# A two-layer hybrid decoder trunk under an offline planner: port lock for more VectorE operations, the silu product on VectorE, every sum of squares as a split pair

## The chip, the core and the metric

The kernel runs on one core of a Trainium2 chip, as one launch. The metric is the device time of that launch in microseconds (us), the median of several runs. The engines are named as the profile names them: PE is TensorE (PEld its weight loads), DVE is VectorE, ACT is ScalarE, POOL is GpSimd and SP is SyncE, which issues all DMAs here.

## What is computed

The trunk has two layers over 1024 positions and a width of 1024, all in float32. A layer normalises, projects into four token mixers (latent attention, gated convolution, causal pooling, sliding-window attention with sinks), normalises each group, projects out, adds, and then runs a SwiGLU feed-forward part. Cut to what the change touches:

```python
def rmsnorm(x, g):
    xf = x.astype(jnp.float32)
    y = xf * lax.rsqrt(jnp.mean(xf * xf, axis=-1, keepdims=True) + RMS_EPS)
    return (y * g.astype(jnp.float32)).astype(x.dtype)
...
for l in range(DEPTH):
    h = rmsnorm(x, attn_norm[l])
    proj = h @ w_in[l]
    ...            # y_a latent attention, y_b conv, y_c pooling, y_d sliding window
    groups = jnp.stack([y_a, y_b, y_c, y_d], axis=2)
    gf = groups * lax.rsqrt(jnp.mean(groups * groups, axis=-1, keepdims=True) + RMS_EPS)
    x = x + (gf.reshape(b, s, D_MIX) * mix_norm[l]) @ w_o[l]
    h2 = rmsnorm(x, ffn_norm[l])
    gate, up = jnp.split(h2 @ w_gate_up[l], 2, axis=-1)
    x = x + (jax.nn.silu(gate) * up) @ w_down[l]
return rmsnorm(x, final_norm)
```

## The kernel before

Activations lie transposed: channels on the 128 partitions, positions along the free axis in two halves of 512 (t = 0 and 1). All SBUF working tiles are halves or pairs of halves out of 47 slots; they are all called `u` in the profile. PSUM tiles (`ps_...`) are 512 float32 wide.

**Products.** Nearly every matmul is done on operands split into two fp32r parts. `split` writes the high part with a cast on ACT (L301) and the low part with a subtraction on DVE (L304); `mm3` (L281) then issues three matmuls for each product: high by high, high by low, low by high. A sum of squares over the channels needs no such product: class `SumSq` squares on ACT (L336, L345), adds on DVE (L353, L347), and `rnorm` multiplies the accumulator by a matrix of ones on PE. That last step is in one of two forms. With `pair=False` the ones and the accumulator are float32 and there is one matmul (L364). With `pair=True` the accumulator is split by L301 and L304, and there are two fp32r matmuls with `ones_r` (L361). What follows is the same: ACT takes logarithm, exponential and square (L370 to L372), DVE one Newton step (L373, L376).

**Stages of a layer.** The input projection feeds the sliding-window units, the convolution and the pooling; then the latent attention with the output projection between its heads; then `combine`, which makes the seven operands of a Strassen-like product for the feed-forward part (Winograd's form: seven half-size products in place of eight). Per block of 128 hidden channels the gate-up part makes sums of weight quarters on POOL (`sums`, L1234 to L1236, `sum4`, L1264), products on PE, and `silu(g, r)`: the sigmoid-weighted gate on ACT (L1477), and its product with the row scale r on POOL (L1479). Results go through DRAM (`ad`, `qd`), and the down part runs the seven products again, with weight sums by `dn_sum` (L1557) on POOL. `premake` (L770 to L773) makes the weight sums of two gate-up blocks early: eight POOL additions in each layer, while the sliding-window units run.

**A sliding-window unit** (`swa_unit`) is a chain through the engines: scores on PE (L594), bias and row minimum on DVE (L604), exponential on ACT (L617), three short DVE operations on the row sums (L627, L629, L630), the scaling of the probabilities on DVE (L632), transposes on PE (L643), and the product with the values (L655).

**What sets the order.** `scheduled_kernel` records the program, gives each instruction a modelled duration (`Order.costs`), and lists it on five queues, one for each engine and one for the DMAs. `_forward` plays the queues against each other; `find` makes a first order, `_search` tries random changes of rank and keeps one when the mean over four draws of DMA delays falls (1500 tries). The order found is imposed on each engine's queue; between engines only the true dependences hold. Buffers and PSUM banks are given out by the planned times, in five rounds. One rule in `_forward` is for the port that DVE and POOL share: an operation of kind `TWO` (DVE) or `POOL` starts once the lock is free, and holds it until about its end. Which DVE operations are of kind `TWO` is said in `Order.kinds`; before the change these are additions and products of two wide SBUF operands:

```python
two = op == "TensorTensor" or op == "TensorScalarPtr" and i.is_scalar_tensor_tensor
if e == "DVE" and two and len(aps) == 2:
    return 0 if any(a.memref.startswith("ps_") for a in aps) else TWO
```

Of the kernel before, what the change touches and what calls it, by code (L numbers as in the profile page):

```python
# [23 lines left out]
P = 128  # L24
D = 1024
# [105 lines left out]
def trunk_kernel(ctx: ExitStack, tc: tile.TileContext, ins, out, given=None, spans=None, made=None):  # L131
# [256 lines left out]
    x_in = ins["xT"]  # L388
    ss = SumSq(D)
    hh = [[None, None] for _ in range(NK)]  # L390
# [48 lines left out]
    for l in range(L):  # L439
# [254 lines left out]
        def group_scale(g):  # L694

            sg = SumSq(2 * P, g in "b")
            for t in range(2):
                for c in range(2):
                    sg.add(t, F.ap(y[g][c][t]))
                r = sg.rnorm(t)  # L700
                for c in range(2):
                    a = F.ap(y[g][c][t])
                    mul_to(a, a, F.ap(r))
                F.free(r)
# [137 lines left out]
        cq = [[None, None], [None, None]]  # L842
        sq_q = SumSq(2 * P)
        for m in range(2):
# [630 lines left out]
        def silu(g, r):  # L1475
            nonlocal last_silu
            last_silu = act.activation(g, g, AF.Silu)  # L1477
            behind(last_silu, ss2.last)
            pool.tensor_tensor(out=g, in0=g, in1=r, op=ALU.mult)  # L1479

# [397 lines left out]
def _forward(eng, kind, seen, taken, kb, want, late, hop, start, to, sync, count, rank, fixed, order):  # L1878
# [21 lines left out]
    for _ in range(n):  # L1900
# [45 lines left out]
        if kind[k] >= TWO:  # L1946
            get = max(t + 0.08, lock)
            more = get - t - 0.08
            lock = get + seen[k] - (0.16 if kind[k] == TWO else 0.19)
        elif e == ACT and want[k] >= 0:  # L1950
            if want[k] != table:
                more = 0.0 if kind[k] == TABLE else 1.29
                table = want[k]
# [68 lines left out]
@compiled  # L2022
def _trials(arrays, graph, lates, order):

    eng, kind, seen, taken, kb, want, hop = arrays
    start, to, sync, count = graph[:4]
    none = np.zeros(0)
    total = 0.0
    for s in range(lates.shape[0]):
        end, _, ok = _forward(  # L2030
            eng, kind, seen, taken, kb, want, lates[s], hop, start, to, sync, count, none, True, order
        )
        if not ok:
            return 1e18
        total += end.max()
    return total / lates.shape[0]


@compiled
def _search(arrays, graph, lates, margin, rank, trials, seed):  # L2040
# [11 lines left out]
    )  # L2052
    best = _trials(arrays, graph, lates, order)
    first = best
# [4 lines left out]
    for it in range(trials):  # L2059
# [57 lines left out]
        if e1.max() > end.max() + 1.5:  # L2117
            continue
        got = _trials(arrays, graph, lates, trial)
        if got < best:  # L2120
# [7 lines left out]
class Order:  # L2128
# [75 lines left out]
    def wide(cls, i):  # L2204
        return [a for a in i.ins if hasattr(a, "memref") and cls.size(a) > 2]

    @classmethod
    def table(cls, i):
# [7 lines left out]
    def kinds(cls, i):  # L2216
# [6 lines left out]
        if op == "TensorTensor" and e == "Pool":  # L2223
            return POOL
        two = op == "TensorTensor" or op == "TensorScalarPtr" and i.is_scalar_tensor_tensor
        if e == "DVE" and two and len(aps) == 2:
            return 0 if any(a.memref.startswith("ps_") for a in aps) else TWO
        return 0

    @classmethod  # L2230
    def costs(cls, i):
# [8 lines left out]
        if e == "PE":  # L2240
            if i.is_transpose:
                return 0.28, 0.109
            if i.ins[0].dtype == F32:
                return n * 0.002, n * 0.0017
            return 0.178 + n * 0.000417, 0.0133 + n * 0.000417
# [44 lines left out]

    def search(self, trials, seed=1):
        rank = self.find()[1]
        best, first, wins, rank, order, begin, end = _search(
# [44 lines left out]
def scheduled_kernel(fresh, ins_of, rounds=5, trials=TRIALS):  # L2338
# [20 lines left out]
    best = None  # L2359
    for _ in range(rounds):  # L2360
        _, _, begin, end = plan.find()
        given = plan.banks(begin, end), plan.spans(made, begin, end)
        nc, traced, made = trace(*given)
        plan = Order(traced, nc.dependency_edges)
        found = plan.find()[0]
        if best is None or found < best[0]:
            best = found, given, plan
    order = best[2].search(trials)[1]
    return trace(*best[1], order)[0]

# [132 lines left out]
```

## Time and profile before

| | before |
|---|---|
| median of 3 runs (lowest, highest) | 2063.58 us (2062.7, 2064.33) |
| the profiled execution, its own time | 2065.29 us |
| span of its instructions | 2063.5 us, 26530 instructions |
| PE busy | 2036.2 us, 9422 matmul records |
| DVE busy | 1564.7 us, 2443 instructions |
| ACT busy | 992.0 us, 1737 instructions |
| POOL busy | 568.5 us, 420 instructions |
| mean granted clock of PE | 0.995 |

The profiled execution is 1.7 us over the median of the runs. A float32 matmul of 512 columns stands in the trace as two records, a fp32r one as one. Matmuls overlap: a record lasts about 0.39 us, while a new one begins every 0.23 us, so the rate is read from the starts or from a count in a window. In the list of waits a row reads: who waited, on which line, for whom; total us, times, longest us. In a timeline a row reads: start, duration, engine, line, operation, tiles, shapes, count, and in brackets the idle time before it and who ended it.

### The profile page before, as it was taken

What the parts mean: (1) busy time and instruction counts of PE and PEld (TensorE: products, weight loads), DVE (VectorE), ACT (ScalarE), POOL (GpSimd) and SP (SyncE); (2) the same over time, 40 slices, a digit from 0 to 9 for tenths busy, and PEclk for the clock granted to TensorE, in tenths of its full rate; (3) what the DMA queues carried; (4) which work ended last, traced back from release to release, by engine and by line L of the source; (5) the groups of instructions that cost most, each with busy time, mean ns of one, the idle gap of its engine ahead of it and who ended that gap; (6) DMA issues with size and microseconds to landing.
All of it is one profiled execution on the core that took longest, in us unless ns stands there. A gap on an engine that the chain in (4) does not pass through costs nothing.

```text
span 2063.5 us, 26530 instructions
## 1 busy us (share of the span) xinstructions
PE 2036.2 (99%) x9422; PEld 1679.0 (81%) x9422; DVE 1564.7 (76%) x2443; ACT 992.0 (48%) x1737; POOL 568.5 (28%) x420
## 2 busy tenths in 40 slices
PE   9999999999999999999999999999999999999998
PEld 7787888778888888888887878888788888888887
DVE  8879978998777678655657899789876767785546
ACT  7447647753333334444434476577433333354332
POOL 0100000037687683000001000000578768710000
PEclk9999999999999999999999999999999999999999
DMA  5301222434555556766403002243355555486542
GB/s 207 128 21 36 76 81 83 160 105 169 183 181 172 182 184 240 260 218 222 160 31 125 31 25 89 67 128 118 109 191 175 184 182 178 165 310 239 186 161 100
DMA packets 142117, 302.36 MB, mean 147 GB/s; under 512 B 13856, under 2 KB 60960, under 8 KB 141984
## 3 DMA queue, kind: packets, MB, share of 16 engines
q1 hardware_dynamic: 141984, 300.66, 43.1%
q8 instruction: 74, 1.21, 0.2%
q14 instruction: 59, 0.48, 0.1%
HBM read 212.00 MB, written 87.56 MB: 145 GB/s over the span
## 4 chain that ended last, share of the span: by engine, by line
PE 87%; DVE 6%; ACT 3%; issue 2%; DMA 1%; POOL 0%; SPq 0%; DVEq 0%; ACTq 0%; POOLq 0%
PE ps_mm L281 34%; PE ps_s L281 26%; PE ps_t L281 10%; PE ps_pv L281 8%; PE ps_pv L1065 2%; PE ps_t L1053 1%; DVE u L304 1%; PE ps_s L999 1%; DVE u L307 1%; PE ps_s L1001 1%; PE ps_s L1000 1%; DMA u<-in_w_gu 1%; PE ps_s L871 1%; PE ps_pv L655 1%; ACT u L306 1%
## 5 line engine op out<-in xcount | busy, mean ns | idle before, releaser
L281 PE MATMUL ps_mm<-u,u 128*128 128x512 f32 (+1 forms) x3378 | 839.3, 391 | 4.2 <-DVE u L304 1.7
L281 PEld LDWEIGHTS ps_mm<-u,u 128*128 128x128 f32 x3378 | 618.5, 189 | 130.9 <-issue 5.4
L281 PE MATMUL ps_s<-u,u 128*128 128x512 f32 x2670 | 639.7, 390 | 3.1 <-ACT u L301 1.0
L304 DVE TENSOR_TENSOR u<-u,u 128x1024 fp32r<-128x1024 f32 (+2 forms) x400 | 477.3, 1210 | 167.7 <-ACT u L301 101.8
L281 PEld LDWEIGHTS ps_s<-u,u 128*128 128x128 f32 x2670 | 500.4, 188 | 112.1 <-ACT u L301 2.6
L301 ACT CAST u<-u 128x1024 fp32r<-128x1024 f32 (+2 forms) x400 | 346.8, 882 | 479.0 <-PE ps_s L281 121.5
L281 PE MATMUL ps_t<-u,u 128*128 128x512 f32 (+1 forms) x1124 | 255.8, 377 | 0.5 <-ACT u L306 0.5
L281 PEld LDWEIGHTS ps_t<-u,u 128*128 128x128 f32 x1124 | 202.7, 188 | 40.3 <-ACT u L306 1.3
L1479 POOL TENSOR_TENSOR tp<-tp,u 128x512 f32<-128x512 f32 x80 | 132.3, 1654 | 338.5 <-ACT tp L1477 338.5
L281 PE MATMUL ps_pv<-u,u 128*128 128x512 f32 x744 | 179.2, 389 | 0.1
L281 PEld LDWEIGHTS ps_pv<-u,u 128*128 128x128 f32 x744 | 139.5, 188 | 29.8 <-ACT tn L1342 0.6
L1062 POOL MEMSET u<- 128x128 f32 x32 | 5.7, 206 | 497.9 <-PE ps_mm L281 324.9
L770 POOL TENSOR_TENSOR u<-u,u 128x512 f32<-128x512 f32 x4 | 5.3, 1316 | 373.1 <-PE ps_s L594 288.1
L1477 ACT ACTIVATE tp<-tp 128x512 f32<-128x512 f32 x80 | 50.5, 632 | 109.1 <-DVE tp L380 108.9
L301 ACT CAST u<-ps_t 128x512 fp32r<-128x512 f32 (+3 forms) x132 | 64.4, 502 | 64.3 <-PE ps_t L643 30.1
L304 DVE TENSOR_TENSOR u<-ps_t,u 128x512 fp32r<-128x512 f32 (+3 forms) x132 | 74.5, 580 | 13.6 <-ACT u L301 12.7
L1264 POOL TENSOR_TENSOR u<-u 128x512 f32<-128x512 f32 x38 | 77.8, 2048 | 20.8 <-DVE u L304 20.8
L306 ACT ACTIVATE u<-u,par 128x512 fp32r<-128x512 f32 x100 | 69.8, 715 | 25.5 <-DVE u L380 11.8
L1557 POOL TENSOR_TENSOR u<-u 128x352 f32<-128x352 f32 x64 | 80.6, 1260 | 2.4 <-DMA u<-in_w_dn 1.3
L307 DVE SCALAR_TENSOR_TENSOR u<-u,par,u 128x512 fp32r<-128x512 f32 x100 | 72.9, 746 | 5.0 <-ACT u L306 4.8
L1557 POOL TENSOR_TENSOR u<-u,u 128x352 f32<-128x352 f32 x64 | 74.6, 1165 | 3.6
L345 ACT ACTIVATE tn<-u 128x512 f32<-128x512 f32 (+1 forms) x91 | 52.3, 595 | 43.3 <-DVE u L1750 41.0
(206 smaller groups left out, 2377.2 us busy)
## 6 DMA issues: line engine op xcount, KB each, us to landing
u<-in_w_gu SPq DMA_DIRECT2D x92, 512.0 KB, 3.6
ad<-u SPq DMA_DIRECT2D x154, 256.0 KB, 2.1
u<-ad SPq DMA_DIRECT2D x70, 512.0 KB, 5.8
u<-in_w_dn SPq DMA_DIRECT2D x64, 352.0 KB, 3.2
qd<-u SPq DMA_DIRECT2D x64, 352.0 KB, 3.0
u<-qd SPq DMA_DIRECT2D x32, 512.0 KB, 5.2
u<-in_w_in SPq DMA_DIRECT2D x28, 512.0 KB, 3.8
u<-in_w_dn SPq DMA_DIRECT2D x24, 512.0 KB, 6.5
```

Source lines behind the costliest of these rows:

```text
L281: pe.matmul(o, w, r, start=start and k == 0 and i == 0, stop=stop and k == n - 1 and i == 2, skip_group_check=again,)
L301: a = act.copy(hi, f)
L304: dve.tensor_tensor(out=lo, in0=f, in1=rd(hi), op=ALU.subtract)
L306: a = act.activation(hi, f, AF.Copy, scale=gain)
L307: dve.scalar_tensor_tensor(out=lo, in0=f, scalar=gain, in1=rd(hi), op0=ALU.mult, op1=ALU.subtract)
L345: act.activation(q, f, AF.Square)
L655: pe.matmul(py[:, (i % 2) * 256 : (i % 2 + 1) * 256], v, R.ap(tt)[:, kb * 256 : (kb + 1) * 256], start=n == 0, stop=n == 2 * nkb - 1,)
L1065: pe.matmul(py[:, c0:], v_of(j, h), R.ap(s)[:, c0:], start=j == 0 and n == 0, stop=j == nj - 1 and n == 1,)
L1264: pool.tensor_tensor(out=q4, in0=q4, in1=F.ap(self.raw[1] + 1), op=ALU.add)
L1477: last_silu = act.activation(g, g, AF.Silu)
L1479: pool.tensor_tensor(out=g, in0=g, in1=r, op=ALU.mult)
L1557: pool.tensor_tensor(out=o, in0=a, in1=b, op=ALU.add)
```

## The change

Three things are changed in what the kernel executes, and the planner around it:

- `SumSq` is built with `pair=True` everywhere: also for the first normalisation, for the groups c and d, and for the latent queries. The one remaining float32 form is the second half of the final normalisation, which `rnorm` takes in two column ranges of 256.
- The product in `silu` is a DVE instruction.
- The planner takes every DVE addition, product, scaling or copy whose tensor operands all lie in SBUF as kind `TWO`, whatever their width; a PE transpose is planned at 0.1135 us where it was 0.109; each of the five rounds is judged by a search of its own, and the last search starts from the best round's ranks. A trial that can no longer win is cut short.

```diff
-    ss = SumSq(D)
+    ss = SumSq(D, True)
...
-            sg = SumSq(2 * P, g in "b")
+            sg = SumSq(2 * P, True)
...
-        sq_q = SumSq(2 * P)
+        sq_q = SumSq(2 * P, True)
...
             behind(last_silu, ss2.last)
-            pool.tensor_tensor(out=g, in0=g, in1=r, op=ALU.mult)
+            dve.tensor_tensor(out=g, in0=g, in1=r, op=ALU.mult)
...
             more = get - t - 0.08
-            lock = get + seen[k] - (0.16 if kind[k] == TWO else 0.19)
+            lock = get + max(0.05, seen[k] - (0.16 if kind[k] == TWO else 0.19))
...
+    @staticmethod
+    def tensors(i):
+        return [a for a in i.ins if hasattr(a, "memref")]
...
-        two = op == "TensorTensor" or op == "TensorScalarPtr" and i.is_scalar_tensor_tensor
-        if e == "DVE" and two and len(aps) == 2:
-            return 0 if any(a.memref.startswith("ps_") for a in aps) else TWO
+        if e == "DVE" and op in ("TensorTensor", "TensorScalarPtr", "TensorScalar", "TensorCopy"):
+            return 0 if any(str(a.memref).startswith("ps_") for a in cls.tensors(i)) else TWO
...
             if i.is_transpose:
-                return 0.28, 0.109
+                return 0.28, 0.1135
...
-    for _ in range(rounds):
+    for r in range(rounds):
         _, _, begin, end = plan.find()
         given = plan.banks(begin, end), plan.spans(made, begin, end)
         nc, traced, made = trace(*given)
         plan = Order(traced, nc.dependency_edges)
-        found = plan.find()[0]
-        if best is None or found < best[0]:
-            best = found, given, plan
-    order = best[2].search(trials)[1]
-    return trace(*best[1], order)[0]
+        found = plan.search(trials // 10, r)
+        if best is None or found[0] < best[0]:
+            best = found[0], given, plan, found[4], found[1]
+    _, given, plan, rank, rows = best
+    found = plan.search(trials, rounds, rank)
+    return trace(*given, found[1])[0]
```

Since the planner runs anew, nearly every row of every queue moves. Three places are shown.

**PE, sliding-window units of layer 0 beside `premake`.** `ps_s` holds a unit's scores, `tp` its probabilities, `ps_t` their transposes; `ps_mm` rows are projection matmuls that need none of it. Before, the scores 884 and 916 are followed by the transposes 903 and 935:

```order
L594 MATMUL ps_s_884<-u27_434,u0_490 128x256
L594 MATMUL ps_s_916<-u27_434,u0_490 128x256
L281 MATMUL ps_mm_952<-u15_156,u35_874 128x512
...
L281 MATMUL ps_mm_952<-u6_218,u35_874 128x512 x2
L281 MATMUL ps_mm_952<-u6_218,u38_875 128x512
L643 MATMUL ps_t_903<-cst_76,tp_893 128x128
L281 MATMUL ps_mm_952<-u19_230,u35_874 128x512
L643 MATMUL ps_t_903<-cst_76,tp_893 128x128 x3
...
L643 MATMUL ps_t_935<-cst_76,tp_925 128x128
```

Between a unit's last score and its first transpose stand 17 matmuls of 512 columns and one of 256 (first unit), and 20 of 512 and four transposes (second). In the changed kernel the same two units are 892 and 924, with transposes 911 and 943:

```order
L594 MATMUL ps_s_892<-u11_442,u14_498 128x256
L281 MATMUL ps_mm_960<-u15_156,u35_882 128x512 x2
...
L594 MATMUL ps_s_924<-u11_442,u14_498 128x256
L281 MATMUL ps_mm_960<-u18_206,u38_883 128x512
...
L281 MATMUL ps_mm_985<-u10_308,u35_882 128x512
L643 MATMUL ps_t_911<-cst_76,tp_901 128x128
...
L643 MATMUL ps_t_943<-cst_76,tp_933 128x128 x4
```

Now 33 matmuls of 512 columns, 12 of 256 and four transposes stand between for the first unit, and 33, 8 and four for the second: they have moved apart, and the second unit's scores lie behind part of the first unit's wait.

**PE, first sum of squares** (half 0 of the first normalisation; `u4_116` is the accumulator, in the changed kernel `u8_254` holds its two parts). Before:

```order
L281 MATMUL ps_s_258<-u16_166,u8_254 128x512 x2
L364 MATMUL ps_t_283<-u4_116,ones_77 128x512
L281 MATMUL ps_s_258<-u16_166,u9_255 128x512
L281 MATMUL ps_s_258<-u17_178,u8_254 128x512 x2
L281 MATMUL ps_s_258<-u17_178,u9_255 128x512
```

In the changed kernel:

```order
L281 MATMUL ps_s_261<-u5_190,u20_257 128x512
L361 MATMUL ps_t_286<-u8_254,ones_r_79 128x512
L281 MATMUL ps_s_261<-u5_190,u20_257 128x512
...
L281 MATMUL ps_s_261<-u7_242,u9_258 128x512
L361 MATMUL ps_t_286<-u8_254,ones_r_79 128x512
L281 MATMUL ps_mm_296<-u21_298,u0_112 128x512
```

One float32 row is now two fp32r rows, a few projection matmuls later than the first stood, with fourteen projection matmuls between the two (the parts are the two halves of one slot, so their names read alike).

**DVE, layer 1, between `combine` and the first gates** (`tp_13061` and `tp_13117` are the same gate of the plain block; the rows around it are `combine`'s). Before:

```order
L380 TENSOR_TENSOR tp_13061<-ps_s_12957,u2_12675 128x512
L1166 SCALAR_TENSOR_TENSOR tp_13070<-u6_11904,par_75,te_13066 128x512
L304 TENSOR_TENSOR u17_13058<-tp_13044,u17_13058 128x512
L304 TENSOR_TENSOR u31_13122<-u20_13119,u16_13121 128x1024
L1153 SCALAR_TENSOR_TENSOR tp_13071<-tp_13070,te_13067 128x512
L304 TENSOR_TENSOR u1_13078<-tp_13070,u1_13078 128x512
L380 TENSOR_TENSOR u0_12519<-ps_t_12958,tp_13061 128x512
```

In the changed kernel:

```order
L380 TENSOR_TENSOR tp_13117<-ps_s_13013,u23_12731 128x512
L1166 SCALAR_TENSOR_TENSOR tp_13126<-u18_11960,par_75,te_13122 128x512
L304 TENSOR_TENSOR u43_13114<-tp_13100,u43_13114 128x512
L304 TENSOR_TENSOR u4_13178<-u22_13175,u37_13177 128x1024
L1153 SCALAR_TENSOR_TENSOR tp_13127<-tp_13126,te_13123 128x512
L304 TENSOR_TENSOR u30_13134<-tp_13126,u30_13134 128x512
L1479 TENSOR_TENSOR tp_13117<-tp_13117,u23_12731 128x512
L304 TENSOR_TENSOR u26_11000<-tp_13127,u20_10988 128x512
L380 TENSOR_TENSOR u15_12575<-ps_t_13014,tp_13117 128x512
```

The product L1479 stands in DVE's own queue, two rows ahead of the operation that uses it; the rows around it are as before. On POOL's queue all 88 rows of L1479 are gone, and no row of another line is.

More of the change, by code (lines that the diff above doesn't have):

```diff
@@ L2022, in _trials @@
 @compiled
-def _trials(arrays, graph, lates, order):
+def _trials(arrays, graph, lates, order, limit):
     eng, kind, seen, taken, kb, want, hop = arrays
@@ L2035, in _trials @@
         total += end.max()
+        if total + (lates.shape[0] - 1 - s) * (limit - 2.0) > lates.shape[0] * limit:
+            return 1e18
     return total / lates.shape[0]
@@ L2052, in _search @@
     )
-    best = _trials(arrays, graph, lates, order)
+    best = _trials(arrays, graph, lates, order, 1e9)
     first = best
@@ L2118, in _search @@
             continue
-        got = _trials(arrays, graph, lates, trial)
+        got = _trials(arrays, graph, lates, trial, best)
         if got < best:
@@ L2289, in find, with search @@
         return best
-    def search(self, trials, seed=1):
-        rank = self.find()[1]
+    def search(self, trials, seed=1, rank=None):
+        if rank is None:
+            rank = self.find()[1]
         best, first, wins, rank, order, begin, end = _search(
```

## The prediction

> **What bounds the kernel now.** I read the page first: busy times and the chain of work that ended last.
>
> ```profile
> span 2063.5 us, 26530 instructions
> PE 2036.2 (99%) x9422; PEld 1679.0 (81%) x9422; DVE 1564.7 (76%) x2443; ACT 992.0 (48%) x1737; POOL 568.5 (28%) x420
> PE 87%; DVE 6%; ACT 3%; issue 2%; DMA 1%; POOL 0%; SPq 0%; DVEq 0%; ACTq 0%; POOLq 0%
> ```
>
> PE is never long without work, so only two things can be won: matmul time itself, and the 27.3 us in which PE is idle (2063.5 - 2036.2). Next, busy time by stretch: the table of windows, whose columns are stretch, length, then busy us and count of PE, PEld, DVE, ACT and POOL.
>
> ```profile
> 90.00:150.00 60.00, 56.31 (x262) 46.33 (x263) 44.87 (x97) 23.26 (x54) 5.75 (x5) 0.94 0.15 54
> 150.00:210.00 60.00, 59.99 (x275) 47.10 (x275) 55.62 (x112) 44.53 (x91) 0.00 (x0) 1.00 0.11 31
> 1170.00:1230.00 60.00, 59.81 (x277) 46.99 (x276) 55.10 (x116) 45.37 (x93) 0.00 (x0) 1.00 0.11 31
> 360.00:440.00 80.00, 77.04 (x327) 60.78 (x326) 75.08 (x114) 55.61 (x90) 4.37 (x3) 0.98 0.36 126
> 1380.00:1460.00 80.00, 76.31 (x328) 60.17 (x328) 75.66 (x113) 56.40 (x91) 6.68 (x3) 1.00 0.35 121
> 500.00:720.00 220.00, 219.87 (x971) 181.78 (x970) 156.15 (x150) 77.03 (x105) 163.50 (x114) 1.00 0.55 180
> 1520.00:1740.00 220.00, 220.00 (x972) 182.16 (x971) 154.93 (x151) 76.33 (x105) 165.91 (x115) 1.00 0.55 182
> ```
>
> The last two rows are the gate-up part, where most silu products are. PE has no gap there: 220 us for 972 matmuls, 0.226 us each. Whatever the product costs on POOL or DVE, this stretch can't get shorter. The idle time lies around the mixers and `combine`. Third, the list of waits of PE alone: it has nineteen rows, which add up to 17.9 us; the first six, one more and the last are
>
> ```profile
> PE ps_t L643 <- DVE tp L632: 7.4, 7, 1.7
> PE ps_mm L281 <- DVE u L304: 1.7, 1, 1.7
> PE ps_pv L497 <- DVE ones L155: 1.1, 1, 1.1
> PE ps_s L281 <- ACT u L301: 1.0, 1, 1.0
> PE ps_s L281 <- DVE u L304: 0.9, 1, 0.9
> PE ps_mm L281 <- DVE u L1283: 0.7, 1, 0.7
> PE ps_t L361 <- DVE u L304: 0.3, 1, 0.3
> PE ps_t L570 <- DVE u L575: 0.2, 1, 0.2
> ```
>
> Most of the rest comes after the last matmul, in the end of the final normalisation, which the change does not touch:
>
> ```profile
> 2053.99 0.70 PE L368 MATMUL ps_s<-tn,ones 128*128 128x256 f32 x2 [0.59 <-ACT tn L367]
> ```
>
> From 2054.69 to the end are 8.8 us. So 17.9 us is all that a better order can win, and 7.4 of it is one wait: transposes of the sliding-window units for their scaled probabilities.
>
> **Term A, the split pairs.** The list of line L364 gives the float32 matmuls of 512 columns, two records each; the timeline of PE gives what one costs and what a pair costs, and the page the length of a matmul record (391 ns):
>
> ```profile
> L364 PE MATMUL ps_t<-u,ones x28: 590/592/697, 19.2 to 1225.1; 128*128 128x512 f32 x28
> ...
> 19.18 1.02 PE L364 MATMUL ps_t<-u,ones 128*128 128x512 f32 x2
> 19.64 2.62 PE L281 MATMUL ps_s<-u,u 128*128 128x512 f32 x9
> ...
> 1015.33 0.62 PE L361 MATMUL ps_pv<-u,ones_r 128*128 128x512 f32 x2
> 1015.79 1.55 PE L281 MATMUL ps_mm<-u,u 128*128 128x512 f32 x6
> ...
> L281 PE MATMUL ps_mm<-u,u 128*128 128x512 f32 (+1 forms) x3378 | 839.3, 391 | 4.2 <-DVE u L304 1.7
> ```
>
> 28 records are 14 sums; in the changed order none of them is left on L364, so all 14 become pairs. One float32 sum: from 19.18 to the end of the nine matmuls behind it (19.64 + 2.62 = 22.26) are 3.08 us; the ninth begins 0.39 earlier, eight starts at 0.226 are 1.81, so 3.08 - 0.39 - 1.81 = 0.88 us. One pair: 1015.79 - 1015.33 = 0.46 us. PE gains 0.42 us each, 14 x 0.42 = **5.9 us**. This is time of PE where PE has no gap, so it comes off the end in full, unless the new operations make PE wait. These are a cast on ACT and a subtraction on DVE for each sum:
>
> ```profile
> 1450.67 0.61 ACT L301 CAST u<-tp 128x512 fp32r<-128x512 f32 x1
> ...
> L304 DVE TENSOR_TENSOR u<-te,u 128x512 fp32r<-128x512 f32 x20 | 13.7, 684 | 1.1 <-ACT u L301 0.9
> ```
>
> The chain from the accumulator to its inverse root grows by 0.61 + 0.68 - 0.42 = 0.87 us. The changed order covers it: the pair stands some matmuls later, and its halves are apart.
>
> **Term B, the lock beside `premake`.** The timeline of 84 to 98 us, DVE, POOL and PE, and the durations of line L632 (least, median, longest):
>
> ```profile
> 89.40 1.26 POOL L773 TENSOR_TENSOR u<-u 128x512 f32<-128x512 f32 x1
> 89.57 2.52 DVE L632 TENSOR_SCALAR tp<-tp,sm 128x256 f32<-128x256 f32 x2
> 90.61 1.32 POOL L770 TENSOR_TENSOR u<-u,u 128x512 f32<-128x512 f32 x1
> 90.95 0.30 PE L643 MATMUL ps_t<-cst,tp 128*128 128x128 f32 x1 [1.58 <-DVE tp L632]
> ...
> 93.48 2.58 DVE L632 TENSOR_SCALAR tp<-tp,sm 128x256 f32<-128x256 f32 x2
> 94.86 0.45 PE L643 MATMUL ps_t<-cst,tp 128*128 128x128 f32 x1 [1.70 <-DVE tp L632]
> ...
> L632 DVE TENSOR_SCALAR tp<-tp,sm x64: 277/347/1429, 53.6 to 1192.1; 128x256 f32<-128x256 f32 x56, 128x128 f32<-128x128 f32 x8
> ```
>
> A scaling takes 0.35 us, and up to 1.43 while POOL adds: it ends just after the addition does. The old planner's rule did not count L632 among the operations that need the port, so it put 17 and 20 matmuls of cover (17 x 0.226 and a half one, 4.0 us; 4.9 us with the transposes) between scores and transposes. The first unit's chain really ran past 92.09 (89.57 + 2.52), the second's past 96.06. The changed order has 33 full and 12 half matmuls and four transposes: 33 x 0.226 + 12 x 0.12 + 4 x 0.11 = 9.3 us, and 8.9 us for the second, whose scores now start later. The additions of `premake` are still there, eight in each layer, but PE has other work. I take the whole row as won, **7.4 us**; the bounds are 0 (the waits turn up at another place of the same stretch) and, with the refilling of PE after each of seven waits at 0.17 (0.39 - 0.226), 8.6.
>
> The row comes first: 1.43 against 0.35. The Trainium skill, "SBUF — State Buffer", section "SBUF: two separate sides", says that VectorE and GpSimd share one port pair as an exclusive lock, held for a whole instruction, by VectorE operations in a 2-port mode or with two SBUF inputs. By that rule the lock of the eight additions is not removed by the change, only planned around, and this term could be 0; that is the second case below.
>
> **Term C, the silu product.** Its durations on POOL, the worst one in layer 1 and what came of it (timeline), and the nearest DVE row for its price:
>
> ```profile
> L1479 POOL TENSOR_TENSOR tp<-tp,u x80: 1282/1544/3956, 416.0 to 1840.5; 128x512 f32<-128x512 f32 x80
> L1479 POOL TENSOR_TENSOR u<-u,u x8: 1283/1577/1867, 420.5 to 1477.6; 128x512 f32<-128x512 f32 x8
> ...
> 1452.14 3.96 POOL L1479 TENSOR_TENSOR tp<-tp,u 128x512 f32<-128x512 f32 x1 [11.76 <-ACT tp L1477]
> 1456.13 0.69 DVE L380 TENSOR_TENSOR u<-ps_t,tp 128x512 f32<-128x512 f32 x1 [1.19 <-POOL tp L1479]
> 1457.48 0.73 PE L281 MATMUL ps_s<-u,u 128*128 128x512 f32 x2 [0.91 <-DVE u L304]
> ...
> L380 DVE TENSOR_TENSOR u<-u,te 128x512 f32<-128x512 f32 x16 | 11.0, 687 | 0.1
> ```
>
> At 1452 POOL could not get the port from a DVE that ran without a gap, needed 3.96 us, DVE then stood idle 1.19 us, and PE 0.91 us for the next split. On DVE the product takes 0.69 us in its turn. In layer 0 a like stall exists on a smaller scale (the 0.7 us wait for L1283). I take **1.5 us**; bounds 0 and 6.6, all PE idle time of the two `combine` stretches (77.04 and 76.31 of 80 busy). In the gate-up part it gains nothing, and costs nothing: even if all 44 products of a layer lay in these 220 us, they would add 44 x 0.69 = 30 us to DVE's 156, and 34 would be left, so the cover holds; without it each product would cost PE its 0.69.
>
> **Term D, what DVE gets in addition.** In 150:210 and 1170:1230 lie six new subtractions each (4.1 us) where DVE has 4.4 and 4.9 us left; in 360:440 and 1380:1460 three products each (POOL's x3; 2.1 us) where it has 4.9 and 4.3. It just fits on paper; in practice a late split makes PE wait. If nothing moves away: 2 x (4.1 + 2.1) = 12.4 us lost. If the planner evens it out, 0: 90:150 has DVE at 44.87 of 60. In 150:210 PE waits for nothing although DVE is 93% busy, so I stay near the low end, a quarter: **+3 us**.
>
> Sum for the profiled execution: 2065.29 - 5.9 - 7.4 - 1.5 + 3.0 = 2053.5. It lay 1.7 us over the median of the runs, so the median should be **2052 us**, 0.6% less than 2063.58.
>
> **The rivals.**
> - *The locks come back elsewhere.* Eight additions a layer still exclude DVE for 10.4 us (8 x 1.3), and stall another unit. Only A is left, D and C cancelling: 2063.6 - 5.9 = 2057.7. For it: POOL waits for data alone, the planner can't hold an addition back. Against it: the doubled cover in the order.
> - *The pairs' longer chain lies open.* PE needs the inverse root soon after; 14 x 0.87 = 12 us are lost, against A 5.9 and B 7.4: about 2062, no change. Against it: PE has projections that need no root, and the pairs that are there already (L361) stand in the list of waits once, with 0.3 us.
> - *DVE becomes the bound* in the four full stretches, and B fails too: from the point where DVE gets over 60 and 80 us of work there, each further us is PE idle; -5.9 + 12.4 gives 2070, slower than before. The Trainium skill, "Perfetto Trace Analysis", section "Optimizing Scalar/DVE Operations", speaks for it: with a saturated VectorE, work may go to GpSimd, and the change does the reverse; by it the sum is this rival's. The trace has DVE at 94% there, but at 71% in the gate-up part.
> - *The change does not do what it says*: excluded by the order, where L1479 has left POOL and the 14 float32 rows are gone.
>
> **How the numbers follow.** Forecast 0.63 (own range 2047 to 2057: B between 8.6 and 5, D between 0 and 6); locks elsewhere 0.20; open chain 0.09; DVE bound 0.08. The low end of the range takes A, B and C near their bounds with D at 0 (2063.6 - 5.9 - 8.6 - 4 = 2045); the high end reaches past the second case to 2061. About 0.2% (4.1 us) can be told from no change, so faster means under 2059.5: 0.60 + 0.17 + 0.03 = 0.80; the same 0.13; slower 0.07.
>
> **What would show it.** A: L364 gone but for the 256-column rows, 14 more pairs on L361, PE busy about 6 us less. B: the wait of L643 for L632 under 2 us, while L632 still has instances of 1.2 us or more. C: no POOL row over 2.3 us around 416 to 440 and 1436 to 1460. D: waits of PE for L304 and L353 in 150:210 and 1170:1230. Wrong it would be if new waits of PE outside these stretches add up to more than 8 us, or if the gate-up part shows any.

## The result, and the profile after

| | before | changed |
|---|---|---|
| median of 4 runs each (lowest, highest) | 2063.32 us (2062.7, 2064.33) | 2053.57 us (2052.52, 2054.1) |
| the profiled execution, its own time | 2065.29 us | 2054.1 us |
| span of its instructions | 2063.5 us | 2052.3 us |
| mean granted clock of PE | 0.995 | 0.999 |

The ratio is 0.9952, with a 95% interval of 0.9934 to 0.9969: the change makes the kernel 9.75 us faster. The page after, its span, its busy times and the chain of work that ended last:

```profile
span 2052.3 us, 26548 instructions
PE 2029.3 (99%) x9422; PEld 1673.9 (82%) x9422; DVE 1556.5 (76%) x2545; ACT 998.5 (49%) x1751; POOL 427.8 (21%) x332
PE 81%; DVE 13%; ACT 3%; issue 2%; DMA 1%; POOL 0%; SPq 0%; DVEq 0%; ACTq 0%; POOLq 0%
```

The span fell by 11.2 us: PE is busy 6.9 us less (2036.2 to 2029.3) and idle 4.3 us less (27.3 to 23.0). The list of waits of PE has 18 rows in place of 19 and adds up to 13.6 us in place of 17.9. Its first four rows and the sixth follow, and then what the lists of single lines say of L632, L364, L361 and L1479 (count, then least, median and longest duration in ns, then first and last start):

```profile
PE ps_mm L281 <- DVE u L224: 2.3, 2, 1.9
PE ps_pv L655 <- DVE u L304: 2.0, 1, 2.0
PE ps_mm L281 <- DVE u L304: 1.8, 2, 1.1
PE ps_s L281 <- DVE te L1685: 1.3, 1, 1.3
...
PE ps_t L281 <- DVE u L1202: 0.8, 1, 0.8
...
L632 DVE TENSOR_SCALAR tp<-tp,sm x64: 277/348/1444, 59.9 to 1179.8; 128x256 f32<-128x256 f32 x56, 128x128 f32<-128x128 f32 x8
...
L364 PE MATMUL ps_s<-u,ones x4: 377/377/378, 2024.9 to 2041.8; 128*128 128x256 f32 x4
...
L361 PE MATMUL ps_t<-u,ones_r x52: 389/393/501, 21.2 to 1374.7; 128*128 128x512 f32 x52
L361 PE MATMUL ps_pv<-u,ones_r x14: 389/391/469, 397.9 to 2012.8; 128*128 128x512 f32 x14
...
L1479 DVE TENSOR_TENSOR tp<-tp,u x80: 677/692/1779, 412.6 to 1829.9; 128x512 f32<-128x512 f32 x80
L1479 DVE TENSOR_TENSOR u<-u,u x8: 679/684/1561, 431.5 to 1462.9; 128x512 f32<-128x512 f32 x8
```

The wait of L643 for L632 is gone, while L632 still has instances of 1.44 us: the lock is there, PE has other work. L364 holds only the 256-column rows, and the 66 records of L361 are 33 pairs. The windows after:

```profile
90.00:150.00 60.00, 57.98 (x289) 48.13 (x288) 46.92 (x107) 26.58 (x65) 5.11 (x4) 1.00 0.20 69
150.00:210.00 60.00, 60.00 (x279) 47.69 (x277) 59.41 (x121) 46.84 (x93) 0.00 (x0) 1.00 0.09 27
210.00:360.00 150.00, 147.10 (x760) 121.73 (x760) 129.81 (x317) 95.52 (x224) 2.81 (x16) 1.00 0.27 88
360.00:440.00 80.00, 78.94 (x344) 63.76 (x343) 78.57 (x120) 59.42 (x94) 1.58 (x2) 1.00 0.37 126
500.00:720.00 220.00, 219.86 (x969) 181.06 (x968) 153.56 (x174) 75.23 (x103) 126.31 (x92) 1.00 0.54 178
1170.00:1230.00 60.00, 58.82 (x265) 46.64 (x264) 59.18 (x115) 46.16 (x90) 0.34 (x2) 1.00 0.12 36
1380.00:1460.00 80.00, 78.50 (x341) 63.01 (x341) 79.51 (x119) 54.14 (x87) 6.73 (x4) 1.00 0.32 109
1520.00:1740.00 220.00, 219.30 (x962) 179.91 (x961) 155.51 (x174) 74.89 (x103) 128.00 (x93) 1.00 0.53 176
```

Three things are to be seen. The stretch beside `premake` (90 to 150) and the two of `combine` (360 to 440, 1380 to 1460) have more PE work in them, and the clock column has 1.00 where the first two had 0.94 and 0.98. DVE is now busy for 59.4 and 59.2 of 60 us in the two mixer stretches, and 78.6 and 79.5 of 80 beside `combine`. And PE has gaps where it had fewer: 147.10 of 150 (before 149.13), 58.82 of 60 (before 59.81), and 0.14 and 0.70 us in the gate-up part, where there were 0.13 and none.

Of the stretch beside `premake`, the timeline after (start, duration) shows what took the place of the old wait:

```profile
92.83 1.29 POOL L770 TENSOR_TENSOR u<-u,u 128x512 f32<-128x512 f32 x1 [3.80 <-DMA u<-in_w_gu]
...
94.38 2.52 DVE L632 TENSOR_SCALAR tp<-tp,sm 128x256 f32<-128x256 f32 x2
...
96.83 1.27 POOL L773 TENSOR_TENSOR u<-u 128x512 f32<-128x512 f32 x1
96.93 1.72 DVE L487 TENSOR_TENSOR u<-te,u 64x512 fp32r<-64x512 f32 x1
98.68 0.69 DVE L304 TENSOR_TENSOR u<-ps_t,u 128x512 fp32r<-128x512 f32 x1
...
99.42 0.62 PE L655 MATMUL ps_pv<-u,u 128*128 128x256 f32 x3 [2.02 <-DVE u L304]
```

The same four additions (the first and the last are shown) still stretch two scalings to 2.52 us and a subtraction to 1.72; the split that follows is late, and PE waits 2.02 us for it, where before it had waited 1.58, 0.66, 1.70 and 0.38 us for L632.

**A cost that no term of the prediction had.** The clock records of the trace before hold three stretches at half rate ahead of the end. In the windows that follow, each of these three stands behind the window just before it; the last two rows are a place where the clock stayed:

```profile
89.72:93.14 3.42, 1.52 (x7) 0.83 (x7) 3.42 (x3) 0.79 (x4) 3.42 (x3) 1.00 0.48 194
93.14:99.97 6.83, 4.75 (x16) 3.81 (x16) 5.14 (x8) 1.85 (x4) 2.61 (x3) 0.50 0.62 230
431.06:434.47 3.41, 1.78 (x6) 0.59 (x4) 3.41 (x6) 1.87 (x4) 1.39 (x1) 1.00 0.00 0
434.47:437.88 3.41, 2.93 (x7) 2.36 (x8) 3.41 (x6) 0.42 (x1) 0.00 (x0) 0.50 0.43 137
1117.14:1120.55 3.41, 1.57 (x8) 1.28 (x9) 2.75 (x4) 0.59 (x1) 3.15 (x3) 1.00 0.48 181
1120.55:1123.96 3.41, 3.41 (x11) 2.84 (x11) 2.00 (x3) 1.23 (x2) 0.00 (x0) 0.50 0.84 303
1451.64:1455.05 3.41, 1.74 (x7) 1.10 (x7) 3.30 (x5) 1.63 (x3) 2.91 (x1) 1.00 0.11 18
1455.05:1458.46 3.41, 2.50 (x11) 1.79 (x10) 2.33 (x4) 0.40 (x1) 1.05 (x1) 1.00 0.57 213
```

The three begin on one grid: 434.47 - 93.14 is 341.33 us, 100 times 3.413, and 1120.55 - 434.47 is 686.08, 201 times. Each follows a window of that grid in which PE was busy for about half of it or less. The changed kernel has none before 2047.6, in its end; its emptiest window on its own grid kept the clock:

```profile
1477.55:1480.96 3.41, 2.06 (x10) 1.40 (x9) 3.31 (x4) 0.12 (x1) 3.41 (x2) 1.00 0.05 5
1480.96:1484.37 3.41, 3.41 (x17) 2.77 (x16) 2.04 (x4) 0.88 (x2) 1.70 (x2) 1.00 0.73 225
```

In the 13.65 us at half rate PE was busy for 11.10, so the loss there is at most 5.6 us. The Trainium skill, "TensorE: Matmul & The Clock Gate", Part 1, says that the clock gate is either at full or at half rate, and that it goes by a free-running window of 4096 cycles, about 3.4 us: the lengths of 3.41 and 6.83 us here agree. It says that the gate closes after an idle window; in this trace no gap of PE was longer than 1.7 us, and windows that were 44% to 52% busy were enough, so on that the measurement decides.

The books then stand so. From start to start, a float32 sum took 0.88 us and a pair takes 0.47 (two rows of 0.237), so 14 sums save 5.7 us of matmul time. Idle time fell by 4.3, and up to 5.6 came from the clock: 15.6 together, but the span fell by 11.2. Some 4 us are missing. They can't lie in idle time, which is counted already. But a record of 0.39 us hides a start that is up to 0.16 us late, and such lateness, at full clock and against the usual distances of the starts (0.227 us for 512 columns, 0.12 for 256), adds up to some 13 us before and 18 after, an estimate from the starts of all matmuls. The experiments look for who gave what.

### The profile page after: what moved, and what is told of

Read it like the earlier page. It is cut to its first block, busy times and chain, and to the rows that moved or that the text cites. A ratio compares the mean times of both kernels' runs of the same rounds, so it can differ in the third digit from the quotient of the medians.

```text
span 2052.3 us, 26548 instructions
## 1 busy us (share of the span) xinstructions
PE 2029.3 (99%) x9422; PEld 1673.9 (82%) x9422; DVE 1556.5 (76%) x2545; ACT 998.5 (49%) x1751; POOL 427.8 (21%) x332
## 4 chain that ended last, share of the span: by engine, by line
PE 81%; DVE 13%; ACT 3%; issue 2%; DMA 1%; POOL 0%; SPq 0%; DVEq 0%; ACTq 0%; POOLq 0%
PE ps_mm L281 29%; PE ps_s L281 27%; PE ps_t L281 10%; PE ps_pv L281 7%; DVE u L304 3%; PE ps_pv L1065 2%; PE ps_t L1053 1%; DVE u L380 1%; DVE u L307 1%; ACT u L301 1%; PE ps_s L999 1%; PE ps_s L1001 1%; PE ps_s L1000 1%; DVE tn L373 1%; DVE u L376 1%
## 5 line engine op out<-in xcount | busy, mean ns | idle before, releaser
L301 ACT CAST u<-u 128x1024 fp32r<-128x1024 f32 (+2 forms) x414 | 354.1, 873 | 494.5 <-PE ps_s L281 119.6
L304 DVE TENSOR_TENSOR u<-u,u 128x1024 fp32r<-128x1024 f32 (+2 forms) x414 | 453.8, 1113 | 164.1 <-ACT u L301 113.5
L1264 POOL TENSOR_TENSOR u<-u 128x512 f32<-128x512 f32 x38 | 72.2, 1899 | 246.1 <-DVE u L304 144.8
L1234 POOL TENSOR_TENSOR u<-u,u 128x512 f32<-128x512 f32 x38 | 60.3, 1586 | 203.4 <-PE ps_s L281 95.9
L770 POOL TENSOR_TENSOR u<-u,u 128x512 f32<-128x512 f32 x4 | 5.2, 1292 | 405.2 <-PE ps_pv L655 401.4
L304 DVE TENSOR_TENSOR u<-ps_t,u 128x512 fp32r<-128x512 f32 (+3 forms) x132 | 75.2, 580 | 13.1 <-ACT u L301 12.2
L1479 DVE TENSOR_TENSOR tp<-tp,u 128x512 f32<-128x512 f32 x80 | 62.7, 783 | 20.9 <-ACT tp L1477 20.9
```

What stands on the lines that cost most here:

```text
L301: a = act.copy(hi, f)
L304: dve.tensor_tensor(out=lo, in0=f, in1=rd(hi), op=ALU.subtract)
L1234: pool.tensor_tensor(out=F.ap(q + 1), in0=a21, in1=a22, op=ALU.add)
L1264: pool.tensor_tensor(out=q4, in0=q4, in1=F.ap(self.raw[1] + 1), op=ALU.add)
L1479: dve.tensor_tensor(out=g, in0=g, in1=r, op=ALU.mult)
```

## The experiments

Ratios are to the kernel before, run on the same chip; its medians were 2066.28 us for the first four, 2066.06 for the next four, 2066.40 for the three after, and 2067.02 for the last.

| run | median (lowest to highest), us | ratio (95%) | at half clock before the end |
|---|---|---|---|
| e1_short_premake | 2052.93 (2051.93 to 2054.91) | 0.9938 (0.9925 to 0.9950) | none |
| e2_short_silu | 2058.54 (2057.75 to 2059.84) | 0.9965 (0.9953 to 0.9978) | 10.2 us |
| e3_only_pairs | 2063.43 (2060.72 to 2065.75) | 0.9987 (0.9979 to 0.9996) | 13.7 |
| e4_only_product | 2061.06 (2060.45 to 2061.86) | 0.9974 (0.9965 to 0.9983) | 13.7 |
| e5_only_planner | 2049.96 (2048.84 to 2050.77) | 0.9921 (0.9908 to 0.9935) | none |
| e6_old_lock | 2062.44 (2060.29 to 2066.13) | 0.9981 (0.9972 to 0.9990) | 13.7 |
| e7_no_pairs | 2054.54 (2053.70 to 2056.28) | 0.9945 (0.9932 to 0.9957) | none |
| e8_other_draw | 2053.33 (2052.74 to 2055.45) | 0.9940 (0.9927 to 0.9952) | none |
| e9_changed_again | 2052.49 (2049.63 to 2054.48) | 0.9930 (0.9918 to 0.9943) | none |
| e10_no_product | 2052.97 (2051.20 to 2056.16) | 0.9935 (0.9922 to 0.9947) | none |
| e11_planner_other_draw | 2050.73 (2050.36 to 2051.41) | 0.9923 (0.9909 to 0.9936) | 3.4 |
| e12_no_pairs_other_draw | 2051.98 (2049.34 to 2052.87) | 0.9927 (0.9914 to 0.9941) | none |

**What the lock beside `premake` cost in the old order.** The order of before is kept to the last row; only the final program's eight additions are short.

```diff
+            c = slice(0, 16) if SHORT[0] else whole
-            pool.tensor_tensor(out=F.ap(q + 1), in0=a21, in1=a22, op=ALU.add)
+            pool.tensor_tensor(out=q1[:, c], in0=a21[:, c], in1=a22[:, c], op=ALU.add)
... (the other three alike)
-            sp.dma_start(made[:, : 2 * HT], F.ap2(q))
+            sp.dma_start(made[:, : 2 * HT], F.ap2(w1 if SHORT[0] else q))
```

> The kernel before with its own order kept row for row, but the eight weight additions of `premake` on POOL add 16 columns in place of 512 (so each keeps the port for some 0.2 us, not 1.3). It leaves out: the other 496 columns of these sums, which gate-up blocks 1 and 2 of each layer then read as raw weights. Theory (the wait of PE for line L632, 7.4 us, is the port held by POOL): L632's longest instance falls from 1.43 us to about 0.4, the wait of L643 for L632 from 7.4 us to under 1, and the time by 7 to 9 us, to 2054 to 2056. Rival (the units are late because DVE's own row of work is late, POOL only coincides): L632 gets shorter, but PE still waits, and the time stays above 2060.

Measured: 13.35 us less, where the theory had 7 to 9. L632 has no long instance left, nobody waits for it, and the stretch is full at full clock:

```profile
L632 DVE TENSOR_SCALAR tp<-tp,sm x64: 275/346/355, 54.3 to 1178.1; 128x256 f32<-128x256 f32 x56, 128x128 f32<-128x128 f32 x8
...
90.00:150.00 60.00, 60.00 (x299) 49.86 (x298) 45.92 (x115) 27.69 (x69) 1.07 (x4) 1.00 0.17 57
```

So the additions are the cause of the wait, and they cost nearly twice the 7.4 us of its row. The row's own 7.4, up to 1.2 for refilling (7 times 0.17), and what the clock lost behind the stalls in 90 to 100 and 1110 to 1125 (at most 4.1, half of 4.75 and 3.41) make up nearly all of the size. The third half-clock stretch, beside `combine`, went too, though the stalls there are as long (1.7, 1.0, 0.9 and 0.7 us in both lists of waits): on this run's grid the emptiest window in 424 to 434 held 1.94 us of PE work. The stall is the same in both traces: a window laid over it at its worst holds 1.47 us (431.38 to 434.79 before, 423.98 to 427.39 here). So it hung on where the grid fell.

**What the silu product on POOL cost in the old order.** The same for the product:

```diff
-            pool.tensor_tensor(out=g, in0=g, in1=r, op=ALU.mult)
+            c = slice(0, 16) if SHORT[0] else whole
+            pool.tensor_tensor(out=g[:, c], in0=g[:, c], in1=r[:, c], op=ALU.mult)
```

> The kernel before with its own order kept row for row, but the 88 silu products on POOL multiply 16 columns in place of 512. It leaves out: the row scale of the other 496 columns. It gives the most that taking the product off POOL can win without a new order. Theory of the forecast (term C, 1.5 us): 2061 to 2063, with the waits of PE near 431 to 437 and 1453 to 1459 shorter and the gate-up part as before. Rival (the product was worth more: every DVE operation that POOL held up counts): below 2059. Second rival (worth nothing, DVE's own order made those waits): within 0.5 us of 2063.3.

Measured: 7.74 us less, where term C had 1.5 and at most 6.6, so the first rival was right. The wait for L632 stays (7.3 us), as do the two half-clock stretches beside `premake`; the one beside `combine` is gone, and with it 3.4 us of half rate. It is more than the move to DVE can bring, since 16 columns hold the lock for hardly any time and cost DVE nothing either.

**Pairs alone and product alone, with the old planner.**

```diff
-    ss = SumSq(D)
+    ss = SumSq(D, True)
... (groups c and d, and the latent queries, alike)
```

> The kernel before, and of the change only the 14 sums of squares as split pairs; the old planner plans it. Theory (terms add up; PE saves 0.42 us for each sum, in full): 2063.3 - 5.9 = 2057.4, with 1 to 2 us either way for the new plan; PE busy 6 us less; the wait of L643 for L632 still 5 us or more, since the old rule is still there. Rival (the pairs' longer chain lies open on PE): 2061 or more, with waits of PE for L304 or behind L361. Rival (luck of the plan is larger than the terms): anywhere from 2052 to 2064, and the waits say where.

```diff
-            pool.tensor_tensor(out=g, in0=g, in1=r, op=ALU.mult)
+            dve.tensor_tensor(out=g, in0=g, in1=r, op=ALU.mult)
```

> The kernel before, and of the change only the silu product on DVE; the old planner plans it. Theory (term C alone): 2060 to 2063, the wait of L643 for L632 still there at 5 us or more. Rival (DVE is the bound around `combine`, so the product costs more there than it frees): 2064 to 2067, with PE idle in the two `combine` stretches above the 3.0 and 3.7 us of before.

Measured: the pairs alone 2.85 us less, about half of what their matmul time is worth, so the theory of 2057.4 us missed. The product alone 5.22 us less, where its theory had 0.3 to 3.3 below the kernel before, and the rival (slower) is out: with it the second `combine` stretch is full.

```profile
360.00:440.00 80.00, 78.86 (x347) 64.02 (x346) 77.45 (x120) 57.71 (x94) 0.00 (x0) 1.00 0.39 128
1380.00:1460.00 80.00, 80.00 (x352) 65.25 (x351) 77.92 (x119) 58.69 (x94) 1.16 (x1) 1.00 0.35 122
```

These two rows of the product alone stand against 77.04 and 76.31 before, 5.5 us of PE work more. Both kernels still wait for L632 (8.1 and 8.3 us). Each of the two was planned once, so part of either gain may be the luck of its order; no second draw of them was run.

**The planner alone, and the change without the lock rule.** The first is the changed kernel with the pairs and the product taken back; the second is the whole change but for its rule on which DVE operations need the port:

```diff
-        if e == "DVE" and op in ("TensorTensor", "TensorScalarPtr", "TensorScalar", "TensorCopy"):
-            return 0 if any(str(a.memref).startswith("ps_") for a in cls.tensors(i)) else TWO
+        two = op == "TensorTensor" or op == "TensorScalarPtr" and i.is_scalar_tensor_tensor
+        if e == "DVE" and two and len(aps) == 2:
+            return 0 if any(a.memref.startswith("ps_") for a in aps) else TWO
```

> The changed kernel's planner (wider lock rule, search in each round) on the kernel before: silu product still on POOL, the 14 sums still float32. Theory (the rule is what removes the 7.4 us wait, and with it the stretches at half clock): the wait of L643 for L632 under 1.5 us, no half-clock stretch beside `premake`, 6 to 9 us faster than before. Rival (the rule alone can't hold the POOL additions back; it needs the product and the pairs): the wait stays at 4 us or more, and the time within 3 us of before.

> The changed kernel with the old lock rule alone put back in the planner (only additions and products of two wide SBUF operands need the port); pairs, product on DVE and the longer search stay. Theory: the wait of L643 for L632 is back at 5 to 8 us, with half-clock stretches near 95 and 1118 us, and the time is 6 to 10 us above the changed kernel. Rival (the better search finds the cover anyway): within 2 us of the changed kernel.

Measured: the planner alone 16.1 us less, more than the whole change and more than its theory's 6 to 9; the change without the rule 3.6 us less, as its theory had it. The planner alone, page and windows:

```profile
span 2047.1 us, 26523 instructions
PE 2029.8 (99%) x9422; PEld 1675.7 (82%) x9422; DVE 1550.6 (76%) x2443; ACT 992.6 (48%) x1737; POOL 572.5 (28%) x420
...
90.00:150.00 60.00, 59.96 (x300) 49.89 (x300) 48.97 (x126) 28.26 (x71) 4.12 (x4) 1.00 0.17 61
150.00:210.00 60.00, 59.93 (x267) 46.64 (x266) 55.53 (x102) 43.21 (x84) 0.00 (x0) 1.00 0.09 27
210.00:360.00 150.00, 149.50 (x777) 125.17 (x776) 130.17 (x314) 96.29 (x222) 3.08 (x16) 1.00 0.32 102
360.00:440.00 80.00, 78.43 (x338) 62.01 (x337) 75.11 (x113) 56.72 (x91) 11.06 (x7) 1.00 0.30 107
1170.00:1230.00 60.00, 59.82 (x265) 47.21 (x264) 57.48 (x115) 42.18 (x83) 0.34 (x2) 1.00 0.14 40
```

The four mixer stretches lack 0.8 us of PE work together (0.04, 0.07, 0.50, 0.18), where the changed kernel lacks 6.1 (2.02, 0, 2.90, 1.18). Its waits add up to 8.3 us. Without the rule they are 22.6 (in the slowest of its eleven runs, 2066.13 us, which is the one traced), with L643 for L632 back and a single wait of 3.5 us for L672, and the clock falls again behind them:

```profile
PE ps_t L643 <- DVE tp L632: 6.0, 6, 2.2
PE ps_t L643 <- DVE u L672: 3.5, 1, 3.5
...
92.96:96.37 3.41, 0.67 (x3) 0.21 (x2) 3.38 (x5) 0.42 (x2) 3.18 (x3) 1.00 0.38 154
96.37:99.79 3.42, 2.68 (x9) 2.26 (x10) 3.15 (x7) 1.82 (x3) 0.00 (x0) 0.50 0.70 237
```

The lock rule carries most of the gain: of the 12.7 us of the whole change by another draw, on the same chip (0.9940, below), 8.5 are gone without it. Each version has its own order, but two draws of one version were at most 3.7 us apart (below).

**The change without the pairs, without the product, and by another draw.** The first two are the changed kernel with one of the diffs above turned round; in the third only the random numbers of the planner's search differ:

```diff
-        found = plan.search(trials // 10, r)
+        found = plan.search(trials // 10, r + 100)
...
-    found = plan.search(trials, rounds, rank)
+    found = plan.search(trials, rounds + 100, rank)
```

> The changed kernel with the 14 sums of squares as float32 matmuls again. Theory (PE gets 0.42 us each back): PE busy 5 to 6 us more, the time 4 to 7 us above the changed kernel. Rival (the pairs' splits cost DVE as much as PE saves): within 1.5 us of the changed kernel, with fewer waits of PE for DVE in 150 to 210 and 1170 to 1230 us.

> The changed kernel with other random numbers in the planner's searches, nothing else: how much the plan's luck is worth. Theory (the mechanisms set the time): within 2 us of the changed kernel, and the wait of L643 for L632 under 1.5 us again. Rival (luck is as large as the terms): 4 us or more away.

> The changed kernel itself, run beside the others as their yardstick. Theory and rival alike: the ratio of its first timing, 0.995 (0.993 to 0.997), so 9 to 13 us below the kernel before; no half-clock stretch ahead of the last matmul.

> The changed kernel with the silu product back on POOL: new planner and pairs. Theory that has formed (with the planner's rule right, the product is better left on POOL, since DVE is the engine PE waits for): 3 to 5 us below the changed kernel, waits of PE in all under 11 us. Rival (the planner alone was a lucky draw, the product costs nothing): within 1.5 us of the changed kernel.

Measured: without the pairs 0.9945, by another draw 0.9940, on one chip; the changed kernel again 0.9930 (13.9 us, a little more than expected), without the product 0.9935, on another. None of the four can be told from the others: both expectations of several us, for leaving the pairs out and for leaving the product out, missed, and their rivals were right. The other draw lies 2.5 us below the first timing of the changed kernel and 2.1 above the second, by the ratios, so luck is a little larger than its theory allowed and well under its rival's 4; the wait of L643 for L632 is 1.0 us there, as expected. But the pairs do leave their mark. The kernel without the product, which has the pairs, in the mixer stretches:

```profile
90.00:150.00 60.00, 59.10 (x294) 48.69 (x293) 49.23 (x119) 26.78 (x69) 5.08 (x4) 1.00 0.19 68
150.00:210.00 60.00, 59.47 (x274) 47.25 (x272) 58.59 (x115) 47.74 (x94) 0.00 (x0) 1.00 0.08 21
210.00:360.00 150.00, 147.28 (x761) 122.06 (x762) 130.41 (x316) 96.63 (x226) 2.87 (x16) 1.00 0.30 93
1170.00:1230.00 60.00, 58.34 (x263) 46.38 (x262) 59.25 (x116) 43.67 (x86) 0.35 (x2) 1.00 0.12 36
```

PE lacks 5.8 us in these four. Every trace of the whole new planner with the pairs lacks 4.7 to 6.2 us there (6.1, 4.7, 6.2 and 5.8 in the changed kernel, by another draw, again, and without the product; the first and third are one order); every one without them lacks 0.8 to 1.9 (0.8, 1.9, and 1.0 and 1.5 in the two below). By the means, 5.7 against 1.3, the pairs save 5.7 us of matmul time, and 4.4 us of gaps go with them. Of these 4.4, 1.1 lie in 90 to 150, where the changed kernel's 2.0 us behind the additions lie too; in the other three stretches it is 4.3 against 1.0. Under the old rule the traces don't sort so: there these three lack 1.1 and 2.3 us without the pairs, 2.6 and 2.0 with them. One row of the lists of waits goes with it: L224, the low part of a weight, made by DVE, is waited for 2.3 to 2.6 us in the four with the pairs, and 0.4 us at most in the four without. The chain behind the pairs isn't what is late, since L361 itself waits for 0.7 us at most. What fits is that DVE, fuller by their subtractions (58.6 to 59.4 of 60 us in 150 to 210 with them, 55.1 to 56.2 without), is late with other work; no run tested that by itself.

**The draw.** Planner alone, and the change without the pairs, both by other random numbers (the diff just above):

> The planner's part of the change alone, with other random numbers in its searches. Theory (its 16 us are the rule and the room DVE has without the product and the pairs): 13 to 17 us below the kernel before, 1.5 us or more below the changed kernel, PE waits in all under 11 us, none of L643 for L632 above 1.5 us. Rival (luck): level with the changed kernel or above it.

> The changed kernel without the split pairs again, but with other random numbers in the planner's search (as in the run without pairs, nothing is left out of the computation). That run lay 4.6 us above the planner alone, its ratio 0.9945 against 0.9921. Theory: this is the product's own cost (88 products of 0.69 us in DVE's queue, late splits beside combine), and a draw moves the time by 1 us or less: then the ratio is 0.9940 to 0.9950 here too, 2053.5 to 2056 us. Rival: the product costs next to nothing, and the first draw of this version was a poor one: then the ratio comes to 0.9915 to 0.9932, 2049 to 2052 us, within the planner alone's.

Measured: 0.9923 for the planner alone (0.9921 by the first draw), 15.7 us and as its theory had it, and 0.9927 without the pairs, where the first draw had 0.9945. So the 4.6 us between the planner alone and the kernel with the product on DVE were for the most part one draw's order; the rival was right there. The planner alone by the other draw also shows the clock fall once more: a window with 1.31 us of PE work beside `combine`, and half rate right after.

```profile
1435.51:1438.93 3.42, 1.31 (x6) 0.45 (x4) 3.42 (x6) 1.57 (x3) 1.74 (x1) 1.00 0.00 0
1438.93:1442.34 3.41, 3.41 (x8) 2.69 (x9) 2.23 (x4) 0.62 (x1) 2.19 (x1) 0.50 0.47 154
```

The best kernel measured is the planner alone: 0.9921 and 0.9923, against 0.9930 to 0.9952 for the change whole. The intervals of these ratios overlap. On one chip the planner alone was 3.4 us faster than the whole change in one pair of draws, where the ranges of the runs lie apart, and 1.8 us in the other, where they overlap; so by its medians it is some 2 to 3 us better.

## Why the prediction was right, and where it was not

The forecast was 2052 us with its own range from 2047 to 2057; 2053.57 came out. The largest term, B, came by the way that it named. That the sum hit so well was luck: its terms were wrong by more, and errors of some 5 us, in A and in B, stood against each other.

- **Term A** (5.9 us of matmul time) was right in size: 5.7 by the starts, 33 pairs on L361, no 512-column row on L364. The step that failed is "so it comes off the end in full". In the mixer stretches PE is without work for some 4.4 us more with the pairs, under the new planner; with the old one the pairs alone gave 2.85 us. Under the new planner no gain of the pairs could be measured. The second rival, the open chain, did not come: L361 itself waits for 0.7 us at most in any of the four traces with the pairs, so the order did cover the chain; what is late is other work of DVE (L224).
- **Term B** (7.4 us, at most 8.6) had the right place and mechanism and too small a size: with the additions cut to 16 columns the old order is 13.35 us faster. The step that failed is "only two things can be won", matmul time and idle time. The prediction quoted the 0.94 in the clock column of 90 to 150 and put no price on it: the stalls had halved the clock behind them, for 10.2 us beside `premake` in the two layers. In the changed kernel 2.0 us of the term came back as the wait of L655 at 99.42, so the rival that the locks return elsewhere was right by that much; the planner alone shows that they need not (0.04 us lacking in that stretch).
- **Term C** (1.5 us, at most 6.6) was too small for the kernel before: 5.2 us with the old planner, 7.7 with the lock's time taken out. There too the clock had fallen, behind the stall at 434. With the new planner the product on DVE brings no gain that could be measured (0.9930 against 0.9935 with the pairs, 0.9945 and 0.9927 against 0.9921 and 0.9923 without). Why is open: in the two `combine` stretches PE still lacks 4.4 us of work in the planner alone, and as much with the product on DVE and no pairs (4.4 and 4.3). No POOL row over 2.3 us is left around `combine`, as was forecast.
- **Term D** (3 us, from 0 to 12.4) was right in sign, but not in place. DVE is full where it said, at 59.4 and 59.2 of 60, yet PE has no gap in 150 to 210 and lacks 1.18 us in 1170 to 1230, and none of the waits there is for L304 or L353. The larger gaps lie beside these stretches: 2.02 us at 99.42, and 1.94 for L224 at 211.96. It was put down to the products and the subtractions alike; under the new planner the gaps go with the pairs. The gate-up part shows 0.14 and 0.70 us without PE work. By the prediction's own words any wait there would make it wrong; the planner alone (both draws) and the kernel without the product have 220.00 of 220 in both windows, and the five traces with the product on DVE lack 0.2 to 1.7 us there, so some idle time does go with the product there, 0.8 us in the changed kernel.
- **DVE becomes the bound**, the rival on the other side, did not decide: the stretches are full, but what doesn't fit costs 4 to 5 us, not 12.4, and B did not fail. The section of the Trainium skill that the prediction names for this rival does not decide for it either: its next sentence says that moving work between these two engines might not help, since they share a port. The rival came nearer than thought, though: the waits of PE outside the stretches named for C and D that were not there before add up to 6.9 us (2.0 for L655 at 99.42, 1.9 for L224 at 211.96, 1.3 for L1685 at 1480.56, and six under 0.4), against the 8 that would have refuted the forecast, while the 7.4 for L632 went.

What stays open: whether the product or the pairs are worth anything under the new planner, since two draws of one version lie up to 3.7 us apart; why no draw with the pairs filled their gaps; and why some 4 us more of late starts go with the changed kernel.

## What to carry to other kernels

Give a planner the shared lock of every operation that takes it: the planner alone gave 16 us, and without that one rule 8.5 of the gain were gone; no edit to the work itself gave as much. A stall of the matrix engine costs more than its row in the list of waits when it leaves a 3.41 us window half empty, so read the clock column beside the waits and price both. Before keeping an edit that saves time on the bound engine, run it without the better order and the better order without it; here the order alone had the lowest times.

## What the runs showed of the hardware

In fourteen traces there are 13 spells at half clock between 20 and 2040 us. Each follows a window of the 3.413 us grid in which PE was busy for 0.67 to 1.78 us. No such window under 1.7 us kept the clock; some from 1.74 on did (1.74 before, 1.75 in the planner alone, 1.77 and 1.78 in the changed kernel's second trace). So the point lies at about half a window, and between 1.7 and 1.8 the modelled ends of matmuls don't tell it apart. A spell lasts one window or two: two where the first held at most 2.68 us of PE work at its half rate, one where it held 2.93 or more. Where the grid lies differs from run to run, so the same stall may or may not cost a spell.
